# Attention scores two blocks ahead, with TensorE's order written out in groups

## Chip, cores and metric

One core of one Trainium2 chip. The metric is the device time of one execution in microseconds, the median of three runs.

## What is computed

One layer of an encoder block over 512 tokens of 1024 features, in float32. What matters here is the middle of it:

```
h = RMSNorm(x);  z = h @ w_in        # GLU input | q 16x64 | k 4x64 | v 4x64 | gate A | gate B
A = pointwise(silu(LayerNorm(depthwise_conv31(GLU(z)))))
for each block of 128 queries, each head:                 # 4 blocks, 16 heads in 4 groups
    keys = this block and its neighbours                  # 2 or 3 blocks of 128
    logits = q.k / 8 - slope * |t - s|, masked beyond 128
    p = exp(logits - max);  o = p @ v / (sum(p) + exp(sink - max))
B = o @ w_o
x = x + (sigmoid(gate_A) * A + sigmoid(gate_B) * B) @ w_out
x = x + PEER(RMSNorm(x))                                  # most of the time, not touched
```

## The kernel before

`encoder_block` is one program for one core, written with a scheduling library: the program names tiles in rotating buffers, and the library adds the semaphores and orders each engine's instructions when it compiles, by program order among what it expects to be ready. Each engine then runs its own list strictly in that order. A `manual_schedule` region fixes the order of the region's instructions on the engines it names; where instructions from outside the region fall among them stays the scheduler's.

**Three products for one.** A float32 operand is split into a hi half (ACT, line 57) and a lo half, the remainder (DVE or POOL, line 58). `mm3` (lines 60 to 65) then issues three matmuls per tile of the contraction: hi x hi, hi x lo, lo x hi. Nearly all of PE's instructions in a trace therefore carry lines 63 to 65, and are told apart by their tiles.

**Projections** (`proj`, `gate`, lines 166 and 240): SP loads 128 output columns of a weight, ACT makes hi halves, POOL lo halves (DVE for w_o and w_pw), PE issues 24 matmuls of 512 columns into a bank of PSUM (tile `mm`, two buffers). A gate's result is copied by ACT to `sg` (line 242). Of the 16 gate projections 11 are placed ahead of attention, five by `fill(1)` inside it.

**Attention** (`attend`, line 253; called 16 times, group g by block b, lines 327 to 332). Four heads of one group share k and v. For one block:

- scores: for each of four heads three matmuls with 64 rows into a bank `s` (two buffers, line 263), 256 or 384 columns for two or three key blocks; DVE adds the bias, takes the maximum and writes the result to `L` (line 267, one custom instruction);
- softmax: ACT takes the exponentials with their sums (line 275), DVE the reciprocal, and both scale two heads each (lines 283 and 285);
- for each key block: four transposes on PE into `pt` (two buffers, line 290), the split into `ph` (ACT) and `pl` (DVE), and three matmuls of 512 columns into `o` (one bank, line 295);
- the output `o` is split back into `qh` and `ql`, in the place of the queries (line 298).

`make_bias` (line 246) writes one group's bias with four ACT instructions into a single buffer. PE's order is the scheduler's: it interleaves single matmuls of two or three blocks, of the gates and, towards the end, of w_o.

**After attention**: the mean over features by eight float32 matmuls with a tile of ones (tile `ln`, line 337; the trace shows two records for each), the differences (DVE, line 342), squares (ACT, line 344, two buffers), the variance (PE, line 345), root (ACT, line 347), reciprocal and products (DVE, lines 348 and 350), silu and its split. Beside that PE runs the eight w_o projections, whose results DVE multiplies by the sigmoid of gate B (lines 360 and 365), and then the eight w_pw projections. The output projection (line 392) follows.

```
            for g in range(4):
                make_bias(g)
                for b in range(NT):
                    attend(g, b)
                    if b == 1 or (g, b) == (0, 3):
                        fill(1)
```

Of the kernel before, what the change touches and what calls it, by code (L numbers as in the profile page):

```python
# [7 lines left out]
F32 = mybir.dt.float32  # L8
F32R = mybir.dt.float32r
# [8 lines left out]
P = 128  # L18
# [26 lines left out]
def encoder_block(ctx, tc, x, g1, w_in, taps, dwb, lng, lnb, w_pw, sink, w_o, w_out, g2, g2row,  # L45
# [14 lines left out]
    def mm3(ps, ws, ms, first=True, last=True):  # L60
        n = len(ws)
        for i, ((wh, wl), (mh, ml)) in enumerate(zip(ws, ms)):
            PE.matmul(ps, wh, mh, start=first and i == 0, stop=False)  # L63
            PE.matmul(ps, wh, ml, start=False, stop=False)  # L64
            PE.matmul(ps, wl, mh, start=False, stop=last and i == n - 1)  # L65
# [51 lines left out]
    with ExitStack() as fc:  # L117
# [58 lines left out]
        with ExitStack() as ac:  # L176
# [73 lines left out]
                    ACT.activation(bt[:, i, :], dist, AF.Copy, scale=-8.0 * slope)  # L250
                biases[g] = bt

            def attend(g, b):
                k0, k1 = max(0, b - 1), min(NT, b + 2)
                n = (k1 - k0) * P
                c0 = (k0 - (b - 1)) * P
                rows = slice(64 * (g % 2), 64 * (g % 2) + 64)
                gp = g // 2
                cols = slice(b * P, (b + 1) * P)
                L = aw.tile([P, 4, 3 * P], F32, name="L", bufs=3)  # L260
                m = sm.tile([P, 4], F32, name="m")
                for i in range(4):
                    s_ps = psa.tile([P, S], F32, name="s")
                    mm3(s_ps[:, :n], [(qh[rows, gp * 4 + i, cols], ql[rows, gp * 4 + i, cols])],
                        [(kh[rows, gp, k0 * P:k1 * P], kl[rows, gp, k0 * P:k1 * P])])
                    h = 4 * g + i
                    DVE.tensor_tensor_reduce(L[:, i, :n], s_ps[:, :n], biases[g][:, i, c0:c0 + n], 0.125,
                                             sinkt[:, h:h + 1], OP.add, OP.max, m[:, i:i + 1])
                nm = sm.tile([P, 4], F32, name="nm")
                DVE.tensor_scalar(nm, m, -1.0, None, op0=OP.mult)  # L270
                es = sm.tile([P, 4], F32, name="es")
                DVE.tensor_tensor(es, sinkt[:, 4 * g:4 * g + 4], m, op=OP.subtract)
                den = sm.tile([P, 4], F32, name="den")
                for i in range(4):
                    ACT.activation(L[:, i, :n], L[:, i, :n], AF.Exp, bias=nm[:, i:i + 1],
                                   accum_out=den[:, i:i + 1])
                ACT.activation(es, es, AF.Exp)
                DVE.tensor_tensor(den, den, es, op=OP.add)
                rd = sm.tile([P, 4], F32, name="rd")
                DVE.reciprocal(rd, den)  # L280
                for i in range(4):
                    if i % 2:
                        ACT.activation(L[:, i, :n], L[:, i, :n], AF.Copy, scale=rd[:, i:i + 1])
                    else:
                        DVE.tensor_scalar(L[:, i, :n], L[:, i, :n], rd[:, i:i + 1], None, op0=OP.mult)
                o_ps = pso.tile([P, 4, P], F32, name="o")
                for j in range(k1 - k0):
                    pt = psa.tile([P, 4, P], F32, name="pt", bufs=2)
                    for i in range(4):
                        PE.transpose(pt[:, i, :], L[:, i, j * P:(j + 1) * P], ident)  # L290
                    ph = aw.tile([P, S], F32R, name="ph")
                    pl = aw.tile([P, S], F32R, name="pl")
                    split(ph, pl, pt.rearrange("p a b -> p (a b)"), DVE)
                    vcols = slice(gp * P, (gp + 1) * P)
                    mm3(o_ps.rearrange("p a b -> p (a b)"),
                        [(vh[:, k0 + j, vcols], vl[:, k0 + j, vcols])], [(ph, pl)],
                        first=j == 0, last=j == k1 - k0 - 1)
                split(qh[rows, gp * 4:gp * 4 + 4, cols], ql[rows, gp * 4:gp * 4 + 4, cols], o_ps[rows], DVE)

            dtmp = aw.tile([P, 4, 3 * P], F32, name="L", bufs=3)[:, 0, :]  # L300
            POOL.iota(dist, pattern=[[-1, 3 * P]], base=P, channel_multiplier=1,
# [22 lines left out]
            fill(2)  # L324
            glup.close()
            pso = ac.enter_context(tc.tile_pool(name="pso", bufs=1, space=PSUM))
            for g in range(4):
                make_bias(g)
                for b in range(NT):
                    attend(g, b)  # L330
                    if b == 1 or (g, b) == (0, 3):
                        fill(1)
            lnp = ac.enter_context(tc.tile_pool(name="lnp", bufs=2))
            ac_hi, ac_lo = bigtile(), bigtile()
            mu_ps = pso.tile([P, S], F32, name="ln")
            for k in range(KD):
                PE.matmul(mu_ps, ones, cv[:, k, :], start=k == 0, stop=k == KD - 1)
            mu = lnp.tile([P, S], F32, name="rs", bufs=1)
            ACT.activation(mu, mu_ps, AF.Copy)
            var = pso.tile([P, S], F32, name="ln")  # L340
            for k in range(KD):
                DVE.tensor_tensor(cv[:, k, :], cv[:, k, :], mu, op=OP.subtract)
                sq = lnp.tile([P, S], F32, name="sq")
# [481 lines left out]
```

## Time and profile before

| | us |
|---|---|
| median of three runs | 1790.5 (1787.73 to 1791.33) |
| the profiled execution | 1785.7 |
| its span | 1783.8 |
| PE busy | 1725.8 (97%) |
| VectorE (DVE) busy | 1387.3 (78%) |
| GpSimd (POOL) busy | 935.5 (52%) |
| ScalarE (ACT) busy | 772.8 (43%) |

The profile lays one execution out by engine. PE is TensorE's matmuls, PEld its weight loads, SP the queue that issues most DMAs. Matmuls overlap: one begins while the one before it still drains, so durations of matmuls add up to more than the time they take, and the distance from start to start is what a matmul costs. "Idle before" names what ended an idle time. PEclk is the clock that was granted to TensorE, 1.00 being 2.4 GHz and 0.50 being 1.2 GHz.

### The profile page before, as it was taken

To read this page: it belongs to the slowest core of one execution; us is meant where nothing else is said; L and a number is where in the kernel's file an instruction comes from. 1 tells how busy PE (TensorE), PEld (TensorE's weight loads), DVE (VectorE), ACT (ScalarE), POOL (GpSimd) and SP (SyncE) were. 2 spreads that over 40 slices of the span, in tenths; PEclk is the share of its full clock that TensorE was granted. 3 is DMA by queue.
4 is the path that set the end of the run, shared out by engine and by line. 5 is a ranking of instruction groups with operands and counts; after the bars stand their busy time and mean duration, and the time that the engine had idled before them with its cause. 6 is when DMAs were issued, how large, how long until landed. Compare 5 with 4: busy or idle time off the path is not lost.

```text
span 1783.8 us, 25146 instructions
## 1 busy us (share of the span) xinstructions
PE 1725.8 (97%) x8873; PEld 1490.2 (84%) x8873; DVE 1387.3 (78%) x2497; ACT 772.8 (43%) x1377; POOL 935.5 (52%) x741
## 2 busy tenths in 40 slices
PE   6999999999999998998899999999999999999998
PEld 5778877667888888998799999999999999999886
DVE  4999866675535999999848889789878777878974
ACT  4233257883333335665433333333333333333253
POOL 4444431020115535444158878888788877877611
PEclk9999999999999998999899999999999999999999
DMA  4222220024233213979868888898888888888972
GB/s 140 91 95 95 95 71 25 24 83 141 83 119 118 82 43 118 278 245 308 309 241 309 310 317 320 295 324 318 305 333 304 306 331 300 309 323 286 361 256 93
DMA packets 148941, 379.41 MB, mean 213 GB/s; under 512 B 11520, under 2 KB 63760, under 8 KB 148816
## 3 DMA queue, kind: packets, MB, share of 16 engines
q1 hardware_dynamic: 110832, 241.20, 38.8%
q0 software_dynamic: 37120, 134.52, 21.2%
q10 hardware_dynamic: 864, 2.10, 0.3%
q8 instruction: 69, 1.13, 0.2%
q14 instruction: 56, 0.46, 0.1%
HBM read 346.84 MB, written 30.93 MB: 212 GB/s over the span
## 4 chain that ended last, share of the span: by engine, by line
PE 78%; DVE 8%; ACT 2%; DMA 1%; issue 0%; SPq 0%; POOL 0%; ACTq 0%; DVEq 0%
PE hps L65 9%; PE hps L64 9%; PE hps L63 9%; PE acc L64 9%; PE acc L63 9%; PE acc L65 9%; PE mm L65 5%; PE mm L63 5%; PE mm L64 5%; PE gp L619 1%; PE s L63 1%; PE gp L620 1%; DMA vraw<-in_v_dram 1%; PE pt L290 1%; PE s L64 1%; PE s L65 1%
## 5 line engine op out<-in xcount | busy, mean ns | idle before, releaser
L58 POOL TENSOR_TENSOR ulo<-uraw,uhi 128x512 fp32r<-128x512 f32 x256 | 383.2, 1502 | 307.6 <-ACT uhi L57 303.3
L63 PE MATMUL hps<-big,uhi 128*128 128x384 f32 x1024 | 348.1, 340 | 2.2 <-ACT hb L442 2.2
L65 PE MATMUL hps<-big,ulo 128*128 128x384 f32 x1024 | 347.9, 340 | 0.6 <-POOL ulo L58 0.6
L64 PE MATMUL hps<-big,uhi 128*128 128x384 f32 x1024 | 347.6, 339 | 0.0
L63 PE MATMUL acc<-vhi,ph 128*128 128x512 f32 x768 | 300.4, 392 | 12.0 <-ACT vhi L57 12.0
L64 PE MATMUL acc<-vlo,ph 128*128 128x512 f32 x768 | 301.3, 392 | 0.3 <-DVE vlo L58 0.3
L65 PE MATMUL acc<-vhi,pl 128*128 128x512 f32 x768 | 300.3, 391 | 0.0
L58 POOL TENSOR_TENSOR wlo<-wraw,whi 128x512 fp32r<-128x512 f32 x120 | 158.1, 1320 | 202.9 <-ACT whi L57 201.3
L57 ACT ACTIVATE uhi<-uraw 128x512 fp32r<-128x512 f32 x256 | 160.5, 632 | 236.4 <-PE hps L64 154.4
L647 DVE SCALAR_TENSOR_TENSOR row<-row,h2tok 128x1024 f32<-128x1024 f32 x128 | 184.8, 1449 | 71.7 <-DMA row<-in_u_dram,eidx 71.3
L658 DVE SCALAR_TENSOR_TENSOR yacc<-row,dots,yacc 128x1024 f32<-128x1024 f32 x127 | 175.3, 1380 | 67.4 <-DMA row<-in_v_dram,eidx 66.9
L58 DVE TENSOR_TENSOR vlo<-vraw,vhi 128x1024 fp32r<-128x1024 f32 x128 | 193.2, 1509 | 18.0 <-ACT vhi L57 17.9
L640 POOL DMA_INDIRECT row<-in_u_dram,eidx x128 | 184.6, 1442 | 33.1 <-issue 20.1
L57 ACT ACTIVATE ph<-hb 128x384 fp32r<-128x384 f32 x128 | 66.9, 523 | 310.7 <-PE acc L64 299.7
L63 PEld LDWEIGHTS hps<-big,uhi 128*128 128x128 f32 x1024 | 194.1, 190 | 6.5 <-ACT hb L442 2.5
L57 ACT ACTIVATE whi<-wraw 128x512 fp32r<-128x512 f32 x152 | 95.3, 631 | 240.5 <-PE mm L64 127.8
L64 PEld LDWEIGHTS hps<-big,uhi 128*128 128x128 f32 x1024 | 194.5, 190 | 4.2
L65 PEld LDWEIGHTS hps<-big,ulo 128*128 128x128 f32 x1024 | 194.0, 189 | 1.2 <-POOL ulo L58 1.1
L640 POOL DMA_INDIRECT row<-in_v_dram,eidx x128 | 166.3, 1299 | 47.6 <-DVE yacc L658 19.5
L63 PEld LDWEIGHTS acc<-vhi,ph 128*128 128x128 f32 x768 | 144.6, 188 | 40.0 <-ACT vhi L57 12.3
L65 PEld LDWEIGHTS acc<-vhi,pl 128*128 128x128 f32 x768 | 144.8, 189 | 31.1 <-DVE pl L58 0.3
L64 PEld LDWEIGHTS acc<-vlo,ph 128*128 128x128 f32 x768 | 144.7, 188 | 28.2 <-DVE vlo L58 1.8
(222 smaller groups left out, 3157.5 us busy)
## 6 DMA issues: line engine op xcount, KB each, us to landing
uraw<-in_ut_dram SPq DMA_DIRECT2D x128, 512.0 KB, 6.3
vraw<-in_v_dram SPq DMA_DIRECT2D x128, 512.0 KB, 5.2
gates_dram<-st SPq DMA_DIRECT2D x12, 2048.0 KB, 8.5
gt<-gates_dram SPq DMA_DIRECT2D x32, 768.0 KB, 7.2
wraw<-in_w_in_dram SPq DMA_DIRECT2D x44, 512.0 KB, 3.3
wraw<-in_w_query_dram SPq DMA_DIRECT2D x16, 512.0 KB, 3.4
wraw<-in_w_o_dram SPq DMA_DIRECT2D x8, 512.0 KB, 3.2
oraw<-in_w_out_dram SPq DMA_DIRECT2D x16, 256.0 KB, 3.1
```

What stands on the lines that cost most here:

```text
L57: ACT.activation(hi, src, AF.Copy)
L58: lo_engine.tensor_tensor(lo, src, f(hi), op=OP.subtract)
L63: PE.matmul(ps, wh, mh, start=first and i == 0, stop=False)
L64: PE.matmul(ps, wh, ml, start=False, stop=False)
L65: PE.matmul(ps, wl, mh, start=False, stop=last and i == n - 1)
L290: PE.transpose(pt[:, i, :], L[:, i, j * P:(j + 1) * P], ident)
L619: PE.matmul(gp[:, k, :], ohl[:, 0, m, :], oij[:, 0, m, :], start=True, stop=False)
L620: PE.matmul(gp[:, k, :], ohl[:, 1, m, :], oij[:, 0, m, :], start=False, stop=True)
L640: POOL.indirect_dma_start(out=row, out_offset=None, in_=table, in_offset=bass.IndirectOffsetOnAxis(ap=eidx[:, c:c + 1], axis=0))
L647: DVE.scalar_tensor_tensor(row, row, 1.0, h2tok, op0=OP.mult, op1=OP.mult, accum_out=dots[:, c:c + 1])
L658: DVE.scalar_tensor_tensor(yacc, row, dots[:, c:c + 1], yacc, op0=OP.mult, op1=OP.add)
```

## The change

`attend` is cut into three functions: `scores(n)` (bias, scores, softmax), `trans(n)` (transposes and their split) and `weigh(n)` (weighted values and the split of the output), with n counting the 16 blocks. In a region that fixes PE's order alone they are called as trans(n), scores(n + 2), weigh(n), with the first two blocks' scores ahead. `piecewise` issues a gate projection in three pieces of nine, nine and six matmuls: four pieces go ahead of the rounds, one follows each odd round up to 13, two follow rounds 14 and 15. `ph` and `pl` move to another pool with three buffers, the third key block's transposes go to a bank `px`, which the mean and the variance use too, and the mean of the layer norm is taken ahead of round 14. The same matmuls are issued in all.

```diff
--- before.py
+++ after.py
@@ -250,21 +250,27 @@
                     ACT.activation(bt[:, i, :], dist, AF.Copy, scale=-8.0 * slope)
                 biases[g] = bt
 
-            def attend(g, b):
+            order = [(g, b) for g in range(4) for b in range(NT)]
+            live = {}
+
+            def span(g, b):
                 k0, k1 = max(0, b - 1), min(NT, b + 2)
-                n = (k1 - k0) * P
+                return k0, k1, (k1 - k0) * P, slice(64 * (g % 2), 64 * (g % 2) + 64), g // 2, slice(b * P, (b + 1) * P)
+
+            def scores(n):
+                g, b = order[n]
+                if b == 0:
+                    make_bias(g)
+                k0, k1, w, rows, gp, cols = span(g, b)
                 c0 = (k0 - (b - 1)) * P
-                rows = slice(64 * (g % 2), 64 * (g % 2) + 64)
-                gp = g // 2
-                cols = slice(b * P, (b + 1) * P)
                 L = aw.tile([P, 4, 3 * P], F32, name="L", bufs=3)
                 m = sm.tile([P, 4], F32, name="m")
                 for i in range(4):
                     s_ps = psa.tile([P, S], F32, name="s")
-                    mm3(s_ps[:, :n], [(qh[rows, gp * 4 + i, cols], ql[rows, gp * 4 + i, cols])],
+                    mm3(s_ps[:, :w], [(qh[rows, gp * 4 + i, cols], ql[rows, gp * 4 + i, cols])],
                         [(kh[rows, gp, k0 * P:k1 * P], kl[rows, gp, k0 * P:k1 * P])])
                     h = 4 * g + i
-                    DVE.tensor_tensor_reduce(L[:, i, :n], s_ps[:, :n], biases[g][:, i, c0:c0 + n], 0.125,
+                    DVE.tensor_tensor_reduce(L[:, i, :w], s_ps[:, :w], biases[g][:, i, c0:c0 + w], 0.125,
                                              sinkt[:, h:h + 1], OP.add, OP.max, m[:, i:i + 1])
                 nm = sm.tile([P, 4], F32, name="nm")
                 DVE.tensor_scalar(nm, m, -1.0, None, op0=OP.mult)
@@ -272,7 +278,7 @@
                 DVE.tensor_tensor(es, sinkt[:, 4 * g:4 * g + 4], m, op=OP.subtract)
                 den = sm.tile([P, 4], F32, name="den")
                 for i in range(4):
-                    ACT.activation(L[:, i, :n], L[:, i, :n], AF.Exp, bias=nm[:, i:i + 1],
+                    ACT.activation(L[:, i, :w], L[:, i, :w], AF.Exp, bias=nm[:, i:i + 1],
                                    accum_out=den[:, i:i + 1])
                 ACT.activation(es, es, AF.Exp)
                 DVE.tensor_tensor(den, den, es, op=OP.add)
@@ -280,22 +286,41 @@
                 DVE.reciprocal(rd, den)
                 for i in range(4):
                     if i % 2:
-                        ACT.activation(L[:, i, :n], L[:, i, :n], AF.Copy, scale=rd[:, i:i + 1])
+                        ACT.activation(L[:, i, :w], L[:, i, :w], AF.Copy, scale=rd[:, i:i + 1])
                     else:
-                        DVE.tensor_scalar(L[:, i, :n], L[:, i, :n], rd[:, i:i + 1], None, op0=OP.mult)
-                o_ps = pso.tile([P, 4, P], F32, name="o")
+                        DVE.tensor_scalar(L[:, i, :w], L[:, i, :w], rd[:, i:i + 1], None, op0=OP.mult)
+                live[n] = L
+
+            def trans(n):
+                k0, k1, w, rows, gp, cols = span(*order[n])
+                L = live[n]
+                live[n] = []
                 for j in range(k1 - k0):
-                    pt = psa.tile([P, 4, P], F32, name="pt", bufs=2)
+                    pt = (psa.tile([P, 4, P], F32, name="pt", bufs=2) if j < 2 else
+                          pso.tile([P, 4, P], F32, name="px"))
                     for i in range(4):
                         PE.transpose(pt[:, i, :], L[:, i, j * P:(j + 1) * P], ident)
-                    ph = aw.tile([P, S], F32R, name="ph")
-                    pl = aw.tile([P, S], F32R, name="pl")
+                    ph = lnp.tile([P, S], F32R, name="ph", bufs=3)
+                    pl = lnp.tile([P, S], F32R, name="pl", bufs=3)
                     split(ph, pl, pt.rearrange("p a b -> p (a b)"), DVE)
-                    vcols = slice(gp * P, (gp + 1) * P)
-                    mm3(o_ps.rearrange("p a b -> p (a b)"),
-                        [(vh[:, k0 + j, vcols], vl[:, k0 + j, vcols])], [(ph, pl)],
-                        first=j == 0, last=j == k1 - k0 - 1)
+                    live[n].append((ph, pl))
+
+            def weigh(n):
+                k0, k1, w, rows, gp, cols = span(*order[n])
+                vcols = slice(gp * P, (gp + 1) * P)
+                o_ps = pso.tile([P, 4, P], F32, name="o")
+                mm3(o_ps.rearrange("p a b -> p (a b)"),
+                    [(vh[:, k, vcols], vl[:, k, vcols]) for k in range(k0, k1)], live.pop(n))
                 split(qh[rows, gp * 4:gp * 4 + 4, cols], ql[rows, gp * 4:gp * 4 + 4, cols], o_ps[rows], DVE)
+
+            def piecewise(i):
+                ws = weights(w_in[28 + i])
+                ps = psm.tile([P, S], F32, name="mm")
+                for k0, k1 in ((0, 3), (3, 6), (6, KD)):
+                    mm3(ps, ws[k0:k1], hT[k0:k1], k0 == 0, k1 == KD)
+                    if k1 == KD:
+                        ACT.activation(sg[i // KD][:, i % KD, :], ps, AF.Copy)
+                    yield
 
             dtmp = aw.tile([P, 4, 3 * P], F32, name="L", bufs=3)[:, 0, :]
             POOL.iota(dist, pattern=[[-1, 3 * P]], base=P, channel_multiplier=1,
@@ -324,20 +349,32 @@
             fill(2)
             glup.close()
             pso = ac.enter_context(tc.tile_pool(name="pso", bufs=1, space=PSUM))
-            for g in range(4):
-                make_bias(g)
-                for b in range(NT):
-                    attend(g, b)
-                    if b == 1 or (g, b) == (0, 3):
-                        fill(1)
             lnp = ac.enter_context(tc.tile_pool(name="lnp", bufs=2))
             ac_hi, ac_lo = bigtile(), bigtile()
-            mu_ps = pso.tile([P, S], F32, name="ln")
-            for k in range(KD):
-                PE.matmul(mu_ps, ones, cv[:, k, :], start=k == 0, stop=k == KD - 1)
-            mu = lnp.tile([P, S], F32, name="rs", bufs=1)
-            ACT.activation(mu, mu_ps, AF.Copy)
-            var = pso.tile([P, S], F32, name="ln")
+            pieces = (None for i in gates for _ in piecewise(i))
+
+            def some(n):
+                for _ in range(n):
+                    next(pieces, None)
+
+            with tc.manual_schedule(engines={mybir.EngineType.PE}):
+                scores(0)
+                scores(1)
+                some(4)
+                for n in range(len(order)):
+                    if n == len(order) - 2:
+                        mu_ps = pso.tile([P, 4, P], F32, name="px").rearrange("p a b -> p (a b)")
+                        for k in range(KD):
+                            PE.matmul(mu_ps, ones, cv[:, k, :], start=k == 0, stop=k == KD - 1)
+                        mu = lnp.tile([P, S], F32, name="rs", bufs=1)
+                        ACT.activation(mu, mu_ps, AF.Copy)
+                    trans(n)
+                    if n + 2 < len(order):
+                        scores(n + 2)
+                    weigh(n)
+                    some({0: 0, 2: 0, 4: 0, 6: 0, 8: 0, 10: 0, 12: 0, 14: 2, 15: 2}.get(n, 1))
+                some(15)
+            var = pso.tile([P, 4, P], F32, name="px").rearrange("p a b -> p (a b)")
             for k in range(KD):
                 DVE.tensor_tensor(cv[:, k, :], cv[:, k, :], mu, op=OP.subtract)
                 sq = lnp.tile([P, S], F32, name="sq")
```

## Rows read from the trace of the kernel before

**Rows 1.** Busy time (instructions) by engine in two stretches, granted clock, DMA share, GB/s

```profile
core 0: us, PE busy (x) PEld busy (x) DVE busy (x) ACT busy (x) POOL busy (x), PEclk, DMA share, GB/s
...
243.20:383.00 139.80, 137.40 (x638) 95.99 (x638) 93.11 (x289) 113.44 (x274) 9.05 (x7) 1.00 0.07 23
...
412.00:479.00 67.00, 67.00 (x294) 54.89 (x294) 30.59 (x47) 17.62 (x28) 0.00 (x0) 1.00 0.28 95
```

**Rows 2.** One tile's instructions (mm): duration min/median/max ns, first and last start us

```profile
L63 PEld LDWEIGHTS mm<-ohi,qh x64: 187/188/192, 479.0 to 523.2; 128*128 128x128 f32 x64
```

**Rows 3.** Groups by line, PE, 243.2 to 479.1: busy us, mean ns, idle before

```profile
L63 PE MATMUL mm<-qh,whi 128*128 128x512 f32 x64 | 27.2, 426 | 3.9 <-DVE sg L365 3.9
...
L64 PE MATMUL s<-kl,qh 64*128 64x384 f32 x32 | 11.1, 346 | 0.0
...
L64 PE MATMUL s<-kl,qh 64*128 64x256 f32 x32 | 9.1, 284 | 0.0
...
L337 PE MATMUL ln<-cv,ones 128*128 128x512 f32 x16 | 8.2, 606 | 0.0
```

**Rows 4.** PE in order of time: start us, us from first start to last end, instruction

```profile
243.90 0.28 PE L65 MATMUL s<-kh,ql 64*128 64x256 f32 x1
244.11 0.50 PE L63 MATMUL mm<-big,whi 128*128 128x512 f32 x1
244.45 0.40 PE L64 MATMUL mm<-big,whi 128*128 128x512 f32 x1
244.77 0.38 PE L63 MATMUL s<-kh,qh 64*128 64x256 f32 x1
245.00 0.28 PE L64 MATMUL s<-kl,qh 64*128 64x256 f32 x1
245.12 0.28 PE L65 MATMUL s<-kh,ql 64*128 64x256 f32 x1
...
246.80 0.33 PE L65 MATMUL s<-kh,ql 64*128 64x384 f32 x1
246.97 0.33 PE L63 MATMUL s<-kh,qh 64*128 64x384 f32 x1
...
297.02 0.60 PE L290 MATMUL pt<-ident,L 128*128 128x128 f32 x4
...
363.49 0.38 PE L63 MATMUL s<-kh,qh 64*128 64x256 f32 x1
...
382.82 3.72 PE L345 MATMUL ln<-sq,ones 128*128 128x512 f32 x8
```

**Rows 5.** DVE in order of time, behind attention

```profile
391.70 3.35 DVE L348 RECIPROCAL rs<-rs 128x512 f32<-128x512 f32 x1 [5.26 <-ACT rs L347]
...
395.69 5.61 DVE L350 TENSOR_TENSOR cv<-cv,rs 128x512 f32<-128x512 f32 x7
```

**Rows 6.** Busy time in a stretch, columns as in rows 1

```profile
400.00:410.00 10.00, 7.29 (x21) 4.87 (x20) 9.12 (x16) 8.39 (x15) 0.00 (x0) 0.72 0.16 53
```

**Rows 7.** ACT in order of time, last eight blocks

```profile
324.96 1.28 ACT L360 ACT_TABLE_LOAD   x1
326.26 3.62 ACT L360 ACTIVATE sg<-sg 128x4096 f32<-128x4096 f32 x1
...
358.56 0.59 ACT L57 ACTIVATE qh<-o 64x512 fp32r<-64x512 f32 x1 [2.11 <-PE o L65]
...
383.01 0.59 ACT L57 ACTIVATE qh<-o 64x512 fp32r<-64x512 f32 x1 [0.67 <-PE o L65]
```

**Rows 8.** Groups by line, ACT and DVE, 243.2 to 383, columns as in rows 3

```profile
L57 ACT ACTIVATE ph<-pt 128x512 fp32r<-128x512 f32 x40 | 22.1, 592 | 12.6 <-PE pt L290 12.4
L275 ACT ACTIVATE L<-L,nm 128x384 f32<-128x384 f32 x32 | 19.3, 608 | 1.8 <-DVE nm L270 1.7
...
L283 ACT ACTIVATE L<-L,rd 128x384 f32<-128x384 f32 x16 | 9.0, 606 | 0.1
...
L58 DVE TENSOR_TENSOR pl<-pt,ph 128x512 fp32r<-128x512 f32 x40 | 26.2, 685 | 17.9 <-ACT ph L57 17.8
L267 DVE CUSTOM_DVE_ANT_0 L<-s,bias,sinkt 128x384 f32<-128x384 f32 x32 | 18.9, 612 | 8.0 <-PE s L65 8.0
```

## Prediction

> **What bounds the kernel now.** I read the busy time of stretches first, then the groups by line, then PE's instructions in order of time, then those of DVE and ACT. The stretch in question begins at 243.2 us, where the first attention score is issued, and ends at 479.0, where the first weights of the output projection are loaded [rows 2]: 235.8 us. PE counts as busy for 137.40 of the 139.80 us of attention itself [rows 1], so by busy time nothing is to be had. That share misleads: a matmul that is held up counts as a longer one. What tells is the time from one start to the next.
>
> Unit costs: 294 matmuls of 512 columns in 67.0 us make 0.228 us each [rows 1]. A score matmul takes 0.117 with 256 columns (245.00 to 245.12) and 0.174 with 384 (246.80 to 246.97). A transpose takes 0.11: four last 0.60 and one alone 0.27, so three steps are 0.33. A float32 statistics matmul takes 0.43: eight last 3.72, the last of them some 0.7 [rows 4].
>
> Counts come from the code and agree with the groups [rows 3]. 512 columns: five gates, eight w_o and eight w_pw projections of 24 each and 120 for the weighted values, 624 in all, 142.3 us. Scores: 96 of 384 columns, 16.7 us, and 96 of 256, 11.2. Transposes: 160, 17.6. Statistics: 32, 13.8. Sum 201.6 us. So 235.8 - 201.6 = **34.2 us are lost**, and the change can win only out of these.
>
> Where they go: (a) **Switches.** A score multiplies 64 rows, everything else 128. From the last score of a run at 243.90, over two 512-column matmuls, to the second score of the next run at 245.00 pass 1.10 us; the units give 0.12 + 0.23 + 0.23 + 0.12 = 0.70. A trip out of the scores and back costs 0.4, one switch 0.2. The order of time has 49 runs of scores, the first ending at 243.90 and the last beginning at 363.49 [rows 4]: 98 switches, 19.6 us. (b) **Behind attention.** The w_o projections wait 3.9 us for the DVE instruction that empties their bank [rows 3]: DVE stands at the reciprocal until 395.05 and runs seven multiplications from 395.69 to 401.30 [rows 5]. From 400 to 410 the granted clock is 0.72, a mean of the levels 1.2 and 2.4 GHz; 21 matmuls took 7.29 us of busy time there where 4.8 would do, 2.5 too many [rows 6]. (c) The rest, some 8 us, is waiting in the last blocks.
>
> **The change, part by part.** *Switches.* The scores of a block become one run, those of blocks 0 and 1 together: 15 runs, 30 switches, 6.0 us in place of 19.6.
>
> *Fixed rounds.* Before, the scheduler puts single gate matmuls wherever PE would wait; now PE meets its groups in one order, and what is behind a waiting group waits too. A round is: transposes of n, scores of n+2, values of n, and on odd n nine or six gate matmuls. PE's own work in rounds 0 to 13: 35 key blocks x 0.44 = 15.4 for transposes, 7 x 2.09 + 7 x 1.40 = 24.4 for scores, 35 x 0.684 = 23.9 for values, 57 gate matmuls = 13.0, switches 5.6; together 82.3, or **5.9 us a round**. This is the lower bound: no waits.
>
> *Upper bound.* There are two score banks for four heads, so the third head waits for DVE's reduction of the first, while DVE also owes block n's lo halves and block n+1's scaling. ACT takes the exponentials of n+2 before it empties the transposes of n+1. The loop from one block's last score to the next block's: a reduction 0.6, small operations 0.4, four exponentials 2.2 to 2.4, the copy of the old output 0.5, two scalings on ACT 1.0, the first hi half 0.6, two or three lo halves 1.5, another reduction and the score behind it 0.9: 7.8 us, with hand-overs **8.1**; the long ones are the means of [rows 8], less what neighbours overlap.
>
> *Taken:* the nearest row is the last four blocks, from the output copy at 358.56 to that at 383.01, 6.1 us a block, where PE had little filler and met the same waits [rows 7]. With the gate share, 13.0/14 = 0.9, this is **7.0 us a round**, an estimate; 1.1 of it is waiting, 15.4 in 14 rounds.
>
> *Ends.* In the prologue 33 gate matmuls (7.5 us) cover nearly all of block 0's softmax: 1.5 us of waiting taken, 0 to 3. Rounds 14 and 15 have no scores ahead, but 30 gate matmuls and the mean's 16 matmuls: 1.0, 0 to 3. The mean uses the bank of the third transpose group, so round 14's third group waits for ACT's copy; that is inside the 1.0.
>
> *Layer norm.* The mean is now taken two rounds before the end, so subtractions and squares can start earlier, and most of w_o's 43.8 us is still ahead of PE when DVE stands at the reciprocal. Of (b) and what goes with it I keep 3.0 us, 0 to 6.
>
> *SP, DMAs, POOL, buffers.* The gates' five weight loads and ten lo halves are the same, only spread; SP issues them between no others that PE waits for, and POOL is busy 9.05 of 139.80 us [rows 1]. Nothing; without that cover a gate's first matmul would wait for a half of some 1.3 us, five times. The third buffers for the halves and the third transpose bank only let a round reach its 7.0.
>
> *Tables.* Before, two sigmoids of 3.62 us fall between the exponentials. The load ahead of one takes 1.28 us and the sigmoid starts 0.02 us behind it [rows 7]. The last B gate now ends in round 14, so both sigmoids leave the attention, and two reloads of the exponential's table go with them: 2.6 us of ACT, beside PE's work, so zero in the sum. The Trainium skill, "ScalarE: Activation LUTs", section "What ACT_TABLE_LOAD costs", counts a drain as well and comes to about 2.66 us a switch. By it ACT would get back 5.3 us, and if ACT set the pace the sum would be lower by up to 2.7 more. The trace shows no such drain, so the rows stand.
>
> **Sum:** 201.6 + 6.0 + 15.4 + 1.5 + 1.0 + 3.0 = 228.5 against 235.8: 7.3 us less. The profiled execution took 1785.7 us, 4.8 below the median 1790.5; it would come to 1778.4, the median to **1783**. Behind 479 us nothing changes and PE goes on without a gap, so the gain should stay.
>
> **Rivals.** *B, the fixed order binds (slower).* Place: the two score banks in each round, where PE may not go on to the values while DVE owes a reduction. At 8.1 us a round 15.4 us come on top: 1798.5. It decides from 7.5 us a round, where the 7.3 are used up. For it: DVE stood 17.8 us for hi halves and 8.0 for scores, ACT 12.4 for transposes, so the engines hand over one by one [rows 8]. Against it: ACT is busy 113.4 us and DVE 93.1 [rows 1]; less sigmoids and four table loads, 12.4, that is 6.3 and 5.8 us a block.
>
> *C, no change.* w_o's matmuls lie outside the region, and the scheduler may still place them inside runs of scores, so that the change does less than it says; or a round comes to 7.3 to 7.7. Then 1787 to 1794.
>
> *D, no waits in the rounds.* 15.4 us less: 1768. For it: PE was without work for only 2.4 us of attention [rows 1]; against it, that was with fillers.
>
> *E, the clock.* From 400 to 410 the clock fell behind the long waits, at a price of 2.5 us [rows 6]. If waits in each round did this: 14 x 2.5 = 35 us, 1818. Against it, the last blocks waited too, and the clock of the whole attention is 1.00 [rows 1]. A section of the Trainium skill speaks for it: "TensorE: Matmul & The Clock Gate", "A second HAM failure mode: psum-queue depth-cycling", by which short idling between groups of matmuls that cycle through banks makes the clock swing. The trace so far bears it out only behind the longer waits.
>
> **How the numbers follow.** A measurement of this kernel can tell some 0.2%, 3.6 us, from no change. Forecast 0.41, D 0.09, C 0.21, B 0.26, E 0.03. Faster is the forecast and D: 0.50; same 0.21; slower B and E: 0.29. The range takes in D's and B's times and leaves out E and what lies beyond them: 1769 to 1799. The forecast's own range is 1776 to 1787.
>
> **What would show it.** Right: 15 runs of scores; about 7.0 us from one output copy to the next; w_o without waits for its bank; the clock at 1.00 throughout. Wrong: the third head's first matmul a microsecond late in every round (B); runs of scores broken by w_o (C); the clock below 1.00 in the rounds (E). The forecast is wrong if a round takes over 7.5 us, or if the waits behind attention stay as they were.

## Result and the profile after

The changed kernel takes **1809.1 us** (median of four runs) where the kernel before takes 1789.9 in the same comparison: ratio 1.0111, interval 1.0086 to 1.0137, so 1.1% slower. The forecast was 1783, with a range of 1769 to 1799. The stretch that the prediction speaks of, from the first attention score to the first weights of the output projection, goes from 235.8 to **253.8 us** (242.6 to 496.4); the profiled execution's span goes from 1783.8 to 1805.5.

The busy time of stretches of the changed kernel; columns as in [rows 1]:

```profile
core 0: us, PE busy (x) PEld busy (x) DVE busy (x) ACT busy (x) POOL busy (x), PEclk, DMA share, GB/s
243.20:383.00 139.80, 121.12 (x534) 92.69 (x533) 83.10 (x274) 90.78 (x249) 8.98 (x7) 0.88 0.05 16
...
242.60:400.60 158.00, 138.76 (x611) 105.12 (x611) 92.57 (x289) 103.86 (x267) 8.98 (x7) 0.89 0.05 17
400.60:496.40 95.80, 94.35 (x399) 74.50 (x398) 52.90 (x77) 46.86 (x70) 11.62 (x8) 1.00 0.35 121
```

In the same 139.8 us PE issued 534 matmuls in place of 638 [rows 1]. It was idle for 18.7 us in place of 2.4, and the granted clock, 1.00 before, is 0.88. Attention now ends at 400.6 with the last output copy instead of 383.0 [rows 7]. Behind it the clock is 1.00 throughout, where [rows 6] had 0.72.

What PE waited for in the changed kernel from 230 to 520 us, PE's own part of the waits (us in total, times, longest):

```profile
PE s L63 <- DVE m L273: 15.6, 24, 2.7
PE o L64 <- DVE pl L58: 3.0, 5, 0.9
PE mm L63 <- DVE sg L402: 1.4, 1, 1.4
PE o L63 <- DVE ql L58: 0.3, 1, 0.3
```

The first row is the score bank: PE may not begin the third or fourth head until DVE has reduced the first or second. The wait of w_o for its bank, 3.9 us in [rows 3], is down to 1.4. One such round in order of time, PE and DVE of the changed kernel:

```profile
309.98 0.60 PE L302 MATMUL px<-ident,L 128*128 128x128 f32 x4
...
310.51 0.38 PE L63 MATMUL s<-kh,qh 64*128 64x256 f32 x1
...
310.81 1.29 DVE L58 TENSOR_TENSOR pl<-pt,ph 128x512 fp32r<-128x512 f32 x2 [0.42 <-ACT ph L57]
...
311.20 0.27 PE L65 MATMUL s<-kh,ql 64*128 64x256 f32 x1
...
312.02 0.68 DVE L58 TENSOR_TENSOR pl<-px,ph 128x512 fp32r<-128x512 f32 x1
...
312.62 0.48 DVE L273 CUSTOM_DVE_ANT_0 L<-s,bias,sinkt 128x256 f32<-128x256 f32 x1
...
313.15 0.38 PE L63 MATMUL s<-kh,qh 64*128 64x256 f32 x1 [1.68 <-DVE m L273]
```

Two heads' scores are there by 311.5. DVE makes three lo halves first, from 310.81 to 312.7, and reduces a head only then; PE's third head starts at 313.15. In the round at 345.8 the fourth head waits 2.7 us in this way.

The clock fell before any long wait. The changed kernel's PE in the first 7 us of attention:

```profile
242.55 0.38 PE L63 MATMUL s<-kh,qh 64*128 64x256 f32 x1
...
243.75 0.38 PE L63 MATMUL s<-kh,qh 64*128 64x256 f32 x1 [0.23 <-DVE m L273]
...
245.96 0.34 PE L65 MATMUL s<-kh,ql 64*128 64x384 f32 x1
246.48 0.69 PE L63 MATMUL s<-kh,qh 64*128 64x384 f32 x1 [0.18 <-DVE m L273]
246.96 0.52 PE L64 MATMUL s<-kl,qh 64*128 64x384 f32 x1
...
249.28 0.63 PE L64 MATMUL mm<-big,whi 128*128 128x512 f32 x1
249.71 0.63 PE L65 MATMUL mm<-big,wlo 128*128 128x512 f32 x1
```

From 242.55 to 246.48 PE issued nothing but scores of two blocks, 64 rows each, with idle times of 0.2 us (0.3 to 0.4 us each by the accounts below). Then a score's 0.34 became 0.52, and a gate matmul, 0.39 at full clock, took 0.63. The kernel before broke the same scores up with gate matmuls [rows 4] and stayed at 1.00. This is the first of eight falls of the clock in the stretch. The other seven stand inside a wait of 0.9 to 2.8 us or within 2 us behind one, so they do not tell idling and kind of work apart.

**Accounts.** For every run below I took PE's matmuls of the stretch from start to start. The unit costs of the prediction, 201.6 us in all and more where a run adds matmuls, are taken off, once more for what was issued while the granted level was the lower one (a gate matmul's step there is 0.43 us, 249.28 to 249.71, for 0.228). A step more than 0.25 us above that is a wait; what is left over is mostly switches. Low clock is the time at the lower level, from the trace's record of levels.

| run | time, us | ratio to before (interval) | stretch | switches | waits | low clock |
|---|---|---|---|---|---|---|
| before | 1789.9 | | 235.8 | 97 | 11.5 | 6.8 |
| changed | 1809.1 | 1.0111 (1.0086 to 1.0137) | 253.8 | 29 | 27.8 | 34.1 |
| e1 reductions first | 1804.1 | 1.0092 (1.0073 to 1.0110) | 249.3 | 29 | 26.8 | 27.3 |
| e2 wait filled, scores | 1814.2 | 1.0148 (1.0131 to 1.0165) | 257.3 | 29 | 19.6 | 34.1 |
| e3 values between heads | 1808.6 | 1.0127 (1.0105 to 1.0149) | 251.0 | 57 | 20.9 | 37.5 |
| e4 free order | 1779.8 | 0.9950 (0.9933 to 0.9967) | 231.9 | 87 | 6.5 | 13.7 |
| e5 wait filled, full size | 1809.0 | 1.0117 (1.0099 to 1.0135) | 251.4 | 57 | 18.4 | 13.7 |
| e6 no lo halves of p | 1790.1 | 1.0007 (0.9996 to 1.0018) | 235.9 | 29 | 16.2 | 20.5 |
| e7 e1, first product repeated | 1805.1 | 1.0098 (1.0078 to 1.0117) | 249.5 | 29 | 14.6 | 10.2 |
| e8 e4, w_o banks emptied first | 1779.5 | 0.9941 (0.9922 to 0.9960) | 231.5 | 87 | 7.2 | 10.2 |
| e9 pieces between heads | 1794.4 | 1.0041 (1.0026 to 1.0056) | 241.3 | 47 | 21.8 | 17.1 |
| e10 e8, w_o lo halves on POOL | 1778.5 | 0.9942 (0.9923 to 0.9961) | 223.1 | 87 | 3.1 | 0.0 |
| e11 fixed order, best parts | 1797.7 | 1.0067 (1.0051 to 1.0084) | 245.4 | 47 | 21.9 | 23.9 |
| e12 before, end edits alone | 1784.9 | 0.9985 (0.9973 to 0.9997) | 230.6 | 95 | 9.9 | 0.0 |

Each ratio is to runs of the kernel before that were taken along with the row's run (medians 1786.9 to 1789.9 us), so ratios compare better across rows than times do. One of e10's six executions, 2868.6 us at a mean granted clock of 0.555, is a slow one and stands neither in its time nor in its ratio; with it the median is 1778.7.

Before against changed: switches and the like 19.9 to 7.7 us, **12 saved**; waits 11.5 to 27.8, **16 lost**; matmuls issued at the lower level 3.2 to 17.1 us' worth, **14 lost**. Together 18, the stretch's growth. Profiles differ by up to 7 us in what they take behind the stretch (1304.8 us before, 1310.5 in e10), so stretch and median do not move quite alike.

### The profile page after: what moved, and what is told of

It reads as the page before. It is cut to its first block, busy times and chain, and to the rows that moved or that the text cites. A ratio compares the mean times of both kernels' runs of the same rounds, so it can differ in the third digit from the quotient of the medians.

```text
span 1805.5 us, 25143 instructions
## 1 busy us (share of the span) xinstructions
PE 1728.2 (96%) x8873; PEld 1500.6 (83%) x8873; DVE 1377.8 (76%) x2497; ACT 768.8 (43%) x1374; POOL 916.2 (51%) x741
## 4 chain that ended last, share of the span: by engine, by line
PE 72%; DVE 10%; ACT 3%; DMA 2%; issue 1%; POOL 1%; SPq 0%; ACTq 0%; DVEq 0%; POOLq 0%
PE hps L63 9%; PE hps L64 9%; PE hps L65 9%; PE acc L64 8%; PE acc L63 8%; PE acc L65 8%; PE mm L63 4%; PE mm L65 4%; PE mm L64 4%; PE gp L656 1%; PE gp L657 1%; DMA vraw<-in_v_dram 1%; DMA row<-in_v_dram,eidx 1%; DVE L L273 1%; DVE rep L494 1%
## 5 line engine op out<-in xcount | busy, mean ns | idle before, releaser
L58 POOL TENSOR_TENSOR ulo<-uraw,uhi 128x512 fp32r<-128x512 f32 x256 | 374.1, 1468 | 287.1 <-ACT uhi L57 281.6
L63 PE MATMUL acc<-vhi,ph 128*128 128x512 f32 x768 | 300.3, 391 | 12.5 <-ACT vhi L57 12.5
L684 DVE SCALAR_TENSOR_TENSOR row<-row,h2tok 128x1024 f32<-128x1024 f32 x128 | 178.2, 1398 | 82.3 <-DMA row<-in_u_dram,eidx 81.7
L695 DVE SCALAR_TENSOR_TENSOR yacc<-row,dots,yacc 128x1024 f32<-128x1024 f32 x127 | 184.0, 1449 | 67.7 <-DMA row<-in_v_dram,eidx 67.5
L58 DVE TENSOR_TENSOR vlo<-vraw,vhi 128x1024 fp32r<-128x1024 f32 x128 | 188.3, 1471 | 20.5 <-ACT vhi L57 20.5
L677 POOL DMA_INDIRECT row<-in_v_dram,eidx x128 | 158.3, 1237 | 49.3 <-DVE yacc L695 20.2
```

The lines of the kernel that those rows point to most:

```text
L58: lo_engine.tensor_tensor(lo, src, f(hi), op=OP.subtract)
L677: POOL.indirect_dma_start(out=row, out_offset=None, in_=table, in_offset=bass.IndirectOffsetOnAxis(ap=eidx[:, c:c + 1], axis=0))
L684: DVE.scalar_tensor_tensor(row, row, 1.0, h2tok, op0=OP.mult, op1=OP.mult, accum_out=dots[:, c:c + 1])
L695: DVE.scalar_tensor_tensor(yacc, row, dots[:, c:c + 1], yacc, op0=OP.mult, op1=OP.add)
```

## Experiments

**e1, reductions first.** Only DVE's order changes: its reductions get ahead of the lo halves.

```diff
-                    DVE.tensor_tensor_reduce(L[:, i, :w], ...)
+                    with tc.high_priority():
+                        DVE.tensor_tensor_reduce(L[:, i, :w], ...)
```

> The changed kernel with one edit: DVE's reductions of the scores get a higher priority when DVE's order is made, so that they stand ahead of the lo halves. PE's order in the region stays. In the changed kernel PE waits 19.4 us between heads of one block for these reductions, and the granted clock is low for 34 us of attention, which costs about 17 us. Theory 1 (the third head waits because DVE makes two or three lo halves first, and the clock falls behind these waits): the waits between heads fall from 19 to under 8 us, the low spells from eight to at most three, time about 1785 (1778 to 1793). Rival (any order of DVE is late somewhere: the lo halves then hold up the weighted values instead): waits move from the heads to the values, the low spells stay six or more, 1803 to 1812.

What PE waited for in e1, 230 to 500 us:

```profile
PE o L64 <- DVE pl L58: 11.3, 18, 1.3
PE s L63 <- DVE m L274: 3.6, 17, 0.3
```

The waits between heads fell as expected, to 6.3 us by the account, but those inside the weighted values rose from 4.3 to 15.6: now the lo halves are late. 1804.1 us and seven low spells are the rival's numbers. DVE's order alone is not the cause; in a fixed round, whichever of the two DVE does second holds PE up.

**e2, the wait filled with scores.** Six score matmuls into the bank of the values, overwritten later; the bank is taken ahead of the scores for that (the lines for it are left out here).

```diff
+                    if i == 2 and idle is not None:
+                        for _ in range(6):
+                            PE.matmul(idle[:, :w], qh[rows, gp * 4, cols], kh[rows, gp, k0 * P:k1 * P],
+                                      start=True, stop=True)
```

> The changed kernel with work added: between the second and the third head of each block from the third on, six more score matmuls whose result is overwritten (14 x 6, 0.7 to 1.0 us a block, in the bank of the weighted values). PE does 12 us more, mostly inside its waits. If the low clock comes from PE's idling in these waits and costs 14 us beyond before, it should vanish or nearly: low time from 34 to under 12 us, time 1795 to 1801 although PE does more. If the clock falls for another reason (the mix of short matmuls and transposes), low time stays near 34 us and the time is 1809 to 1816.

The waits between heads fell from 19.4 to 8.5 us, though 5.9 came back as waits for the values' bank. The low clock stayed at 34.1 us, and the time rose by 5. Filling the wait with more scores did nothing for the clock.

**e3, values between the heads.** The last two rounds, with no scores ahead, keep their place (left out here).

```diff
                 for i in range(4):
+                    if i == 2 and n >= 2:
+                        weigh(n - 2)
                     s_ps = psa.tile([P, S], F32, name="s")
```

> The changed kernel with the weighted values of block n moved between the second and third head of block n+2, so that PE has 1.4 to 2.1 us of work where it waited for the reductions. Cost: 14 more runs of scores, 28 switches of 0.2 us, 5.6 us. Theory 1: waits between heads from 19 to under 5 us, part of it comes back as waits of the values for their halves (their cover falls from four heads to two), low spells at most four; 1785 to 1798. Rival (ACT and DVE are too slow for any such round): the waits only move, 1805 or more.

Waits between heads are nearly gone, 1.1 us, but the values now wait 14.3 us for their halves, which have lost half their cover. 28 more switches cost 4 us. The rival again: most of the waits moved, 20.9 us in place of 27.8. The low clock is 37.5 us, the most of all runs: nine or six full-size matmuls between the heads did not hold it there, where they themselves wait for their halves.

**e4, the free order.** The region is taken away, everything else stays.

```diff
-            with tc.manual_schedule(engines={mybir.EngineType.PE}):
+            with ExitStack():
```

> The changed kernel without the region that fixes PE's order: the same functions in the same program order, pieces, buffers and banks as in the changed kernel, but PE's order is the scheduler's again. If the fixed order is the loss, time returns to that of the kernel before or below it, since the layer norm's part stays better: 1778 to 1790, score waits under 3 us, low spells one or none, 70 to 100 switches. Rival (the loss comes from what else changed: scores two ahead in program order, the shared bank px, gate pieces that hold a bank): 1800 or more.

1779.8 us, 29 less than the changed kernel and 0.5% **below the kernel before**. Its stretches:

```profile
243.30:383.00 139.70, 138.18 (x641) 99.75 (x641) 94.27 (x293) 113.77 (x275) 9.12 (x7) 0.98 0.07 23
383.00:475.20 92.20, 88.99 (x369) 70.72 (x368) 51.16 (x74) 40.34 (x63) 11.88 (x8) 0.96 0.36 120
```

641 matmuls in the time in which the changed kernel issued 534. Two low spells were left, not "one or none". So the loss comes with the fixed order; scores two ahead, the shared bank and the split pieces do not carry it.

**e5, the wait filled with full-size matmuls.** The place of e2, another kind of work (edit against e2).

```diff
-                        for _ in range(6):
-                            PE.matmul(idle[:, :w], qh[rows, gp * 4, cols], kh[rows, gp, k0 * P:k1 * P], ...)
+                        for _ in range(4):
+                            PE.matmul(idle, vh[:, k0, gp * P:(gp + 1) * P], hT_hi[:, 0, :], start=True, stop=True)
```

> The same place as in the run that filled the wait with six score matmuls, but four matmuls of 128 rows and 512 columns instead (0.9 us and two switches, 1.3 us a block; result overwritten). There the waits between heads fell from 19.4 to 8.5 us, yet the low clock stayed at 34.1 us. Theory M (the clock falls because transposes, 64-row scores and short waits stand together for several microseconds; full-size matmuls among them hold it): low time under 14 us, time 1796 to 1806 in spite of 13 x 14/10 = 18 us of added PE work, part of it inside waits. Theory W (the waits alone set the clock): waits fall as with the score matmuls, low time again about 34 us, 1814 to 1824.

The stretch of e2, then that of e5:

```profile
243.40:500.70 257.30, 242.65 (x1093) 192.00 (x1093) 146.54 (x366) 151.19 (x336) 20.26 (x15) 0.93 0.17 56
```

```profile
243.20:494.60 251.40, 238.00 (x1064) 182.29 (x1064) 144.82 (x366) 151.19 (x336) 20.18 (x15) 0.97 0.17 57
```

The waits are alike, 18.4 us in e5 and 19.6 in e2. The low clock is 13.7 us in place of 34.1, in spite of 28 more switches. Both have waits of 1.6 to 1.8 us for the values' bank at three places: in e2 the clock fell at the end of each or within 1 us behind it, in e5 behind one alone. The fillers differ from e2's in rows (128 for 64) and in columns (512 for 256 or 384) at once; which of the two counts was not tried. The time, 1809.0, is above the expected 1796 to 1806: the added 12.8 us of work and the switches eat what the clock gives back.

**e6, less for DVE.** The lo halves of the probabilities are left out, 24 us of DVE's work, and the hi half stands in their place, so that the values come out otherwise; PE's list stays.

```diff
-                    split(ph, pl, pt.rearrange("p a b -> p (a b)"), DVE)
-                    live[n].append((ph, pl))
+                    ACT.activation(ph, pt.rearrange("p a b -> p (a b)"), AF.Copy)
+                    live[n].append((ph, ph))
```

> The changed kernel without the lo halves of the probabilities: DVE's 40 subtractions (0.61 us each, 24 us) are left out and the hi half is used in their place, so PE issues the same matmuls in the same order while its waits for DVE shrink. Theory W (idle waits set the clock): waits from 27.8 to under 12 us, low time from 34 to under 10 us, 1772 to 1782. Theory M (the mix of groups sets it): waits fall alike, low time stays above 24 us, 1787 to 1796.

Between the theories: waits 16.2 us and low clock 20.5 are neither's numbers, the time, 1790.1, is in theory M's range. Fewer waits do lower the low-clock time, but do not end it. Both the waits and the kind of work around them count. Even with 24 us less work for DVE the fixed order is only level with the kernel before.

**e7, the first product repeated.** e1, with full-size matmuls where its waits stand.

```diff
                 o_ps = pso.tile([P, 4, P], F32, name="o")
+                for _ in range(5):
+                    PE.matmul(o_ps.rearrange("p a b -> p (a b)"), vh[:, k0, vcols], live[n][0][0],
+                              start=True, stop=True)
```

> The kernel with reductions first (there 15.6 us of waits stand inside the weighted values, low clock 27.3 us, 1804), with the first product of the values issued five times more in each block, 128 rows and 512 columns, ahead of the accumulation: 16 x 1.14 = 18.2 us of PE work, in the place of the waits for lo halves. Theory M: low time under 10 us, waits inside the values under 4 us, 1796 to 1806. Theory W in this place too (filled waits hold the clock) gives the same; if neither the waits' place nor the size matters, low time stays above 24 us and the time is 1810 to 1822.

PE does 18 us more and the stretch takes 249.5 us in place of 249.3. The low clock falls from 27.3 to 10.2 us and the waits inside the values from 15.6 to 1.7, so here fewer waits and more full-size work go together.

**e8 and e10, the end of attention in the free order.** e8 lets DVE empty w_o's banks ahead of the layer norm; e10 also moves the lo halves of w_o's weights to POOL. Both are built on e4; the edit shown is e10's, e8 keeps `lo_engine=DVE`.

```diff
-                ps = proj(w_o[j], oT, lo_engine=DVE)
-                DVE.tensor_tensor(sg[1][:, j, :], ps, sg[1][:, j, :], op=OP.mult)
+                ps = proj(w_o[j], oT)
+                with tc.high_priority():
+                    DVE.tensor_tensor(sg[1][:, j, :], ps, sg[1][:, j, :], op=OP.mult)
```

> A version meant to beat both: the free order (1779.8), and DVE empties a w_o bank ahead of the layer norm's work in its order. The free order has one wait of 3.2 us of PE for that emptying and a low-clock spell of 6.8 us right behind it. If DVE's order is the cause: wait under 1 us, the spell at the end gone, 1773 to 1778. Rival: the emptying still stands behind the reciprocal, or the layer norm's chain gets late in its place: 1778 to 1784.

> A version meant to beat both: free order, DVE empties w_o's banks first, and POOL, not DVE, makes the lo halves of w_o's weights. In the run before, a wait of 3.7 us for such a half on DVE had taken the place of the wait for the emptying. If DVE's in-order list behind attention is the cause: that wait under 1 us, waits in all under 5 us, 1773 to 1778. Rival: POOL's 1.3 us a half (0.69 on DVE) are late in turn, or the layer norm is the next in line: 1778 to 1784.

In e8 a wait of 3.7 us for a lo half on DVE took the place of the 3.2 us for the bank, and the time did not move: the rival's time, though not by either wait that it named. With POOL in DVE's place both are gone, the clock is 1.00 over the whole stretch, and the stretch is 223.1 us:

```profile
243.50:466.60 223.10, 221.54 (x1009) 166.09 (x1009) 141.02 (x350) 153.22 (x338) 41.77 (x31) 1.00 0.19 64
```

The median, 1778.5, is just above the expected 1778 and not told apart from e8's 1779.5: what lies behind the stretch is 1310.5 us long in that profile, 5.7 more than before's. Both beat both kernels, the one before by 0.6% and the changed one by 1.7%.

**e9, the pieces between the heads.** The fixed order with nothing added; the gate's pieces move.

```diff
+                    if i == 2:
+                        some(pieces_between)
...
-                        scores(n + 2)
+                        scores(n + 2, n % 2)
```

> The changed kernel with nothing added: the gate's pieces move from behind the values to between the second and third head of the scores, one in each odd round, one in each of the first two blocks. PE's order stays fixed; 18 more switches, 3.6 us. If the place of the full-size matmuls is what matters (they stand in the wait and break up the stretch of transposes and scores): waits from 27.8 to under 20 us, low clock from 34 to under 20 us, 1788 to 1799. If only more full-size work holds the clock, as the added matmuls did, low clock stays at 27 us or more and the time is 1803 to 1813.

1794.4 us, 15 below the changed kernel (12.5 by the stretch), with the low clock halved to 17.1 us; the waits, 21.8, are not under the expected 20. The place of the full-size matmuls matters; no more of them were needed. Waits in the even rounds, which have no piece, are left, and 11.8 us of them stand in three rounds, 2, 6 and 10, those whose scores open a new group. There ACT writes three or all four heads' parts of the new bias only behind the round's hi halves, and DVE cannot reduce those heads before. Round 2:

```profile
273.85 0.59 ACT L57 ACTIVATE ph<-px 128x512 fp32r<-128x512 f32 x1
274.33 1.35 ACT L250 ACTIVATE bias<-dist 128x384 f32<-128x384 f32 x3
...
275.30 0.47 DVE L275 CUSTOM_DVE_ANT_0 L<-s,bias,sinkt 128x256 f32<-128x256 f32 x1
...
275.84 0.58 PE L63 MATMUL s<-kh,qh 64*128 64x256 f32 x1 [3.47 <-DVE m L275]
```

All three falls of the clock that e9 has left stand in these three waits or right behind one. In the changed kernel the same rounds hold 6.8 of the 19.4 us between heads. A second buffer for the bias was not tried.

**e11 and e12.** All that helped, in the fixed order (e9 with e1's and e10's edits), and e10's two edits in the kernel before.

> The fixed order with all that helped: pieces between the second and third head, reductions first on DVE, and behind attention w_o's banks emptied first and its lo halves on POOL. Free order with the last two took 1778.7. If the fixed order as such loses (it cannot fill the waits that are left): waits inside attention still 12 us or more, 1783 to 1791. If only its place of the pieces and DVE's order lost: waits under 8 us, low clock under 7 us, 1770 to 1779.

> The kernel before with the two edits behind attention alone (w_o's banks emptied first, lo halves of w_o on POOL). If the free-order version's gain comes from behind attention only: waits of PE for DVE there vanish (3.9 us), the low spell of 6.8 us too, 1778 to 1782. If the mean two blocks early, the sigmoids out of the exponentials and scores two ahead carry part of it: 1782 to 1787.

e11 is no faster than e9 alone: 1797.7 us, outside either expectation, with a stretch 4.1 us longer, though the intervals of the two ratios overlap. With the reductions first 16.1 us of waits stand inside the values, where no piece stands, and the low clock is back at 23.9 us. e12 comes to 1784.9, ratio 0.9985, in the second alternative's numbers by time: its waits for the bank fell to 1.3 us and the low clock to none, and the stretch is 5.2 us shorter, of which the median shows 2. The larger part of e10's gain thus lies in what the change brought beside the fixed order, as e4's 0.9950 without these edits also says. Which of it (the early mean, the sigmoids behind the exponentials, the scores two ahead) was not tried alone.

## Why the prediction was wrong, point by point

**Right: the switches.** 30 were foreseen, 29 counted. What is left over in the accounts after waits and clock falls from 19.9 us at 97 switches to 7.7 at 29: 0.18 us each, against 0.2 from one trip in [rows 4]; e3 with 57 has 11.6 and e4 with 87 has 18.1, near the same line. The Trainium skill, "TensorEngine Tiling (Array Packing)", section "Key Properties", says that changing the tiling mode drains the engine. The trace agrees, with these 0.18 us.

**Right: behind attention.** 3.0 us of waits were kept, 2.8 measured, and the clock's drop there has gone.

**Right, and without effect: the sigmoids.** They left the exponentials. No wait in PE's list above ends with ACT; what ACT delays reaches PE through DVE, which waits for hi halves and bias.

**Wrong: "Taken: 7.0 us a round".** Thirteen rounds lie between the first output copy and the fourteenth. ACT in order of time in the changed kernel:

```profile
266.35 0.58 ACT L57 ACTIVATE qh<-o 64x512 fp32r<-64x512 f32 x1
...
377.07 0.60 ACT L57 ACTIVATE qh<-o 64x512 fp32r<-64x512 f32 x1 [2.25 <-PE o L65]
```

That is 110.7/13 = 8.5 us a round, above even the bound of 8.1. Some 0.95 of it is matmuls at the lower clock, the next point; without that it is about 7.6, over the 7.5 at which the gain is used up. The row that I took it from, the last four blocks of the kernel before, is one of a free order: there the scheduler found matmuls of w_o, of the next block or of the variance for the gaps. PE of the kernel before, with w_o's matmuls (`mm<-q`) between transposes and the weighted values behind them:

```profile
361.56 1.03 PE L290 MATMUL pt<-ident,L 128*128 128x128 f32 x8
362.35 0.48 PE L65 MATMUL mm<-qh,wlo 128*128 128x512 f32 x1
362.66 0.39 PE L63 MATMUL mm<-qh,whi 128*128 128x512 f32 x1
362.89 0.40 PE L64 MATMUL mm<-ql,whi 128*128 128x512 f32 x1
363.13 0.43 PE L63 MATMUL o<-ph,vh 128*128 128x512 f32 x1
```

It prices no round that may not be refilled. Waiting came to 27.8 us in the stretch against the 20.9 of the sum (15.4 + 1.5 + 1.0 + 3.0): 7 us of the miss. The mis-sized term is the 15.4 for rounds 0 to 13, which measured 22.9; prologue, ends and w_o came to 1.1, 1.0 and 2.8, as summed or less. Rival B named place and mechanism rightly, the two score banks with DVE's lo halves ahead of its reductions; the late bias of rounds 2, 6 and 10 it did not name.

**Wrong: the clock left out of the sum, rival E at 0.03.** 17 us of the 25 us by which the stretch exceeds the forecast's 228.5 are matmuls at the lower level. I argued from the granted clock of the whole attention, 1.00 in [rows 1], that short waits do no harm. But that clock came with the free order, which put full-size gate matmuls between the scores; the change takes exactly this away. Nor are long waits a condition, as I had it: at 246.5 us the clock fell in a run of nothing but scores. e2 against e5 shows it with place and waits held: full-size matmuls in a gap left 13.7 us of low clock, scores in the same gap 34.1. e1 against e7 fits this but takes the waits away too, and e6, with the same matmuls in the same order and fewer waits, shows that waits have a share. The Trainium skill, "TensorE: Matmul & The Clock Gate", section "A second HAM failure mode: psum-queue depth-cycling", says that short idling between groups of matmuls that cycle through banks makes the clock swing. The trace now agrees in the swing, with eight falls and 0.88 for 1.00 over the same 139.8 us; that idling alone does it is not borne out by e2 and e5. How much is due to short idling and how much to the kind of work was not separated further.

**Why more than B.** B's 1798.5 was waits alone. Waits and clock together make 1809: a round that waits also ran its matmuls more slowly, and e5 against e2 shows that the second can be lessened with the first left as it is. (The range's lower end, 1769, is 1 us above D's 1768, which the prediction takes to be inside.)

## What to carry to other kernels

A saved switch is worth 0.2 us, and an order that saves 68 of them can still lose: before fixing one, ask for each group what fills PE when the engine behind it is late, and price the group from a stretch with no filler. Where work alternates between full-size and narrow or short matmuls, full-size ones whose operands are ready are worth spreading: moving the same gate pieces into the heads' gap halved the low clock and shortened the stretch by 12.5 us. The values, which had to wait for theirs, did not serve (e3). A clock of 1.00 in the profile before belongs to the order that was there, and is no promise for another.

## What the runs showed of the hardware

A run of 64-row score matmuls 4 us long with idle times of only 0.2 us was followed by the lower clock level. 18 us of added full-size matmuls (e7) cost nothing in the stretch, 249.5 us against e1's 249.3, as waits and low clock fell. And six scores in a gap left the low-clock time at 34.1 us where four full-size matmuls in the same gap left 13.7.
